# First layer's projection: weight quarters, q stores and modulation pieces issued by items of the tile loop

## The chip, the core and the metric

The kernel runs on one core of one Trainium2 chip. The time is the device time of one execution in microseconds; of several runs the median counts. A core has TensorE (PE in the profile, PEld for its weight loads), VectorE (DVE), ScalarE (ACT), GpSimd (POOL) and SyncE (SP), each with its own queue of instructions; SP issues nearly all loads and stores here.

## The reference, cut to what matters

Two layers of a generator work on 1024 latent and 256 context tokens of width 1024. The first is windowed attention, the second latent attention:

```python
for i in range(DEPTH):                       # DEPTH = 2
    shift_x, scale_x, gate_x = adaln(c, ada_w[i], ada_b[i])
    shift_c, scale_c, gate_c = adaln(c_ctx, ada_w[i], ada_b[i])
    hx = rms_norm(x, norm_g[i]) * (1.0 + scale_x[:, None]) + shift_x[:, None]
    hc = rms_norm(ctx, norm_g[i]) * (1.0 + scale_c) + shift_c
    ...
    x = x + gate_x[:, None] * yx

def window_gqa(hx, hc, w_in, ...):
    q, k, v, g = jnp.split(h @ w_in, ...)    # 1024, 256, 256, 1024 columns
    qx = apply_rope(qx, cos, sin)
    kx = apply_rope(kx, cos, sin)
    ...
    yx = (ox * jax.nn.silu(gx)) @ w_out
```

The change lies in the first layer's product `h @ w_in` and in what runs beside it: `silu(c) @ ada_w` for the first layer's gate and for the whole second layer.

## The kernel before, in words

**Split precision.** Each operand of a product is kept as a high and a low part. `split` (L117 to L121) makes them: ACT casts the value to the high part (L120), and VectorE or GpSimd subtracts it for the low part (L121). A product is three matmuls (L125, L126, L127).

**Items.** `w_in` is cut into ten blocks of 256 columns (`blocks`). Block 0 (v) runs first, token pair by token pair. Then a list `order` of items (block, token group, column half) sets the rest. Blocks 1, 3, 5 and 6 are q, block 7 is k, blocks 2, 4, 8 and 9 are the gate. An item with token group 1 or 2 is 24 matmuls of 512 columns; one with group 0 (the context tokens, both halves) is 48 of 256. So a block is five items, written here as 3,0,0, then 3,1,0, 3,1,1, 3,2,0 and 3,2,1. Blocks 1 to 7 run one after another, 8 and 9 interleaved. `proj_t` (from L428) does an item: the matmuls into one of six PSUM banks, then what empties the bank.

**q tiles.** For a q item DVE multiplies the bank by the cosine (L468) and shuffles it (L469), POOL multiplies by the sine (L470) and adds (L472). The function `rest`, called one item later, splits the sum into a staging tile (ACT L120, DVE L121) and stores it with four DMAs (L487). A gate tile is one ACT instruction (L443) and a store (L446, L448).

**Weights.** `fetch(bi)` brings a block's weights: four quarters of 256 KB, each loaded through a ring of three staging buffers (`stg`), then split by ACT and POOL into one of two weight buffers (`wst`). The call for block b+1 is made at block b's first item, all four quarters at once, so the fourth load must wait until POOL has split the first quarter. From here on "quarter 0 to 3 of block 4" names them.

**Modulation.** `ada_vec` is a generator for eight jobs. A job is 512 columns of `ada_w` in eight pieces of 256 KB (128 rows each), 64 pieces in all, loaded through a ring of four buffers (L341). DVE multiplies a piece by the condition and adds it up (L360, L362), once for the token condition and once for the context's; jobs 6 and 7 have only one. A finished job is summed over partitions by PE (`ada_sum`, L373, one or two matmuls), copied by ACT (L377) or added by DVE (L379); for jobs 2 to 5 four transposes on PE follow (`ada_end`, L392), and small additions (L167, L170). One item lies between the last piece and the sum, and one between the sum and the transposes, counted by `later` and `next_item`. One step of the generator was one DVE instruction; the tile loop took 2, 5 or 6 steps per item, and the next load was called in the same step that used the piece's buffer last.

**What sets the order.** The code above is not yet the order on the engines. A scheduler puts each engine's instructions in a fixed order by the dependences between them, and moves loads and DVE work ahead of where the code calls them. On the chip each engine follows its own order, and waits at an instruction until its inputs and its buffer are there.

Of the kernel before, what the change touches and what calls it, by code (L numbers as in the profile page):

```python
# [59 lines left out]
def kernel(ctx: ExitStack, tc: tile.TileContext, t, out, dbg=None):  # L60
    nc = tc.nc
# [11 lines left out]
    q0_d = dpool.tile([4, 64, 2, NT, 512], F32, name="q0_d")  # L73
# [148 lines left out]
    def load_w(dst, src, stage, nk, n, lo_eng=None, col0=0, k0=0):  # L222

        per = max(1, 512 // n)
        for k in range(k0, nk, per):
            st = shp(stage.next(), per, n)
            load(out=st, in_=src[k * 128 : (k + per) * 128, col0 : col0 + n].rearrange("(k p) n -> p k n", p=128))
            split(dst[:, 0, k : k + per, :], dst[:, 1, k : k + per, :], st, lo_eng or nc.gpsimd)
# [37 lines left out]
    blocks = [1280, 0, 1536, 256, 1792, 512, 768, 1024, 2048, 2304]  # L266
    wt = {}

    def fetch(bi, eng=None):
        wt[bi] = r_at(wst[bi % 2], 2, 8, 256)  # L270
        load_w(wt[bi], w_in, stg, 8, 256, lo_eng=eng, col0=blocks[bi])

    def fetch0(h):
        wt[0] = r_at(wst[0], 2, 8, 256)
# [36 lines left out]
        ada0.set_cols(mt[:, :, 32:34], 0, h)  # L311


    due = []
    item = [0]

    def later(d, fn):
        due.append((item[0] + d, fn))

    def next_item():  # L320
        item[0] += 1
        todo = [x for x in due if x[0] <= item[0]]
        due[:] = [x for x in due if x[0] > item[0]]
        for _, fn in todo:
            fn()

    def ada_vec():
        stage = Ring(F, [14, 16, 18, 20], 512)
        acc = Ring(F, [22, 24, 26, 28], 512)
        tmp = Ring(F, [30, 32], 512)  # L330
        for b in tmp.bufs:
            nc.gpsimd.memset(b[0:33], 0.0)
        jobs = [(ada0, 4), (ada0, 5), (ada1, 2), (ada1, 3), (ada1, 0), (ada1, 1), (ada1, 4), (ada1, 5)]
        pieces = [(a, cb, k) for a, cb in jobs for k in range(8)]
        ws = {}

        def fetch_piece(i):
            if i < len(pieces):
                a, cb, k = pieces[i]
                ws[i] = stage.next()  # L340
                load(out=ws[i], in_=t["ada_w"][a.layer, k * 128 : k * 128 + 128, cb * 512 : cb * 512 + 512])  # L341

        for i in range(4):
            fetch_piece(i)
        i = 0
        for a, cb in jobs:
            nw = 1 if a.layer == 1 and cb >= 4 else 2
            accs = [acc.next() for _ in range(nw)]
            m = tmp.next()
            if cb >= 4:  # L350
                for c in range(nw):
                    load(
                        out=m[32 * c : 32 * c + 1],
                        in_=t["ada_b"][a.layer, cb * 512 : cb * 512 + 512].partition_broadcast(1),
                    )
            for k in range(8):
                w = ws.pop(i)
                for c in range(nw):
                    if k == 0:
                        nc.vector.tensor_scalar_mul(accs[c], w, sc[:, k, c : c + 1])  # L360
                    else:
                        nc.vector.scalar_tensor_tensor(accs[c], w, sc[:, k, c : c + 1], accs[c], ALU.mult, ALU.add)  # L362
                    if c == nw - 1:
                        fetch_piece(i + 4)
                    yield
                i += 1
            later(1, lambda a=a, cb=cb, accs=accs, m=m: ada_sum(a, cb, accs, m))

    def ada_sum(a, cb, accs, m):
        ps = pss()  # L370
        n = len(accs)
        for c in range(n):
            nc.tensor.matmul(ps[32 * c : 32 * c + 1], const[:, 0:1], accs[c], start=True, stop=True)  # L373
        for c in range(n):
            r = slice(32 * c, 32 * c + 1)
            if cb < 4:
                nc.scalar.copy(m[r], ps[r])  # L377
# [44 lines left out]
    def proj_t(bi, gp, c):  # L422
# [51 lines left out]
        def rest():  # L474
            q = shp(qst.next(), 2, 512)
            if c0 == 1024:
                for e in range(2):
                    es = slice(64 * e, 64 * e + 64)
                    nc.vector.tensor_add(q[0:64, e], a[es], r[es])
                    kh = kT[:, 2 * c + e, t0 : t0 + 512]  # L480
                    split(kh[0:64], kh[64:128], q[0:64, e])
                return
            split(q[:, 0].bitcast(F32R), q[:, 1].bitcast(F32R), a)
            for e in range(2):
                for s in range(2):
                    o0 = e * 256 + c * 128
                    load(  # L487
                        out=q0_d[c0 // 256, :, s, t0 // 128 : t0 // 128 + 4, o0 : o0 + 128],
                        in_=shp(q[64 * e : 64 * e + 64, s], 4, 128),
                    )  # L490

        return rest

# [189 lines left out]
    def steps(g, n=200):  # L683
        for _ in range(n):
            next(g, None)
# [61 lines left out]
    for bi, gp, c in order:  # L747
        if bi + 1 < 10 and bi + 1 not in started:
            started.add(bi + 1)
            fetch(bi + 1)  # L750
        next_item()
        steps(ada_steps, 200 if (bi, gp) == (8, 0) else 6 if blocks[bi] >= 1536 else 2 if gp else 5)
        if (bi, gp, c) == (9, 2, 0):
            load2(out=mask, in_=t["mask"])
            load2(out=gx, in_=gate_d[0, 0, :].partition_broadcast(128))
            load2(out=gc, in_=gate_d[0, 1, :].partition_broadcast(128))
        if (bi, gp) == (8, 0):
            units[0].prep_q()
            units[0].prep()
            units[1].prep_q()  # L760
        if (bi, gp) == (9, 0):
            units[1].prep()
            units[2].prep_q()
            for h in range(4):
                units[0].score(h)
        r = proj_t(bi, gp, c)
        if rest:
            rest()
        rest = r
        if bi >= 8 and gp != 1:  # L770
            for _ in range(2):
                next(wo_fill, None)

    units[1].score(0)
    units[1].score(1)
    tq = iter([(u, c) for u in units for c in range(u.m)])
# [755 lines left out]
```

## Time and profile before

| | |
|---|---|
| runs | 1644.03 us median of 3 (1641.09 to 1647.05) |
| profiled execution | 1647.77 us, of it the span 1645.9 us |
| mean granted clock of TensorE | 0.99 |
| busy shares | PE 96%, DVE 59%, ACT 50%, POOL 48% |
| matmuls at L125, L126, L127 | 608.1, 599.2 and 597.0 us busy |
| modulation on DVE (L362) | 98 instructions, 87.7 us |
| read and written in HBM | 129.04 MB and 46.15 MB, 106 GB/s over the span |

Times in rows of the profile are counted from the start of the span. A row of a timeline gives start, length, engine, line and operation, the tile written and the tiles read, and in brackets how long the engine had been idle before and what ended that. `arena_f` and `arena_r` are the two large arrays on chip, in which all buffers lie; `PB` is PSUM.

### The profile page before, as it was taken

The numbers are of one execution on the slowest core, as the hardware profiler recorded it, in microseconds if no ns is written. First come the engines' busy times: TensorE is split into PE (matmuls) and PEld (weight loads), VectorE is DVE, ScalarE is ACT, GpSimd is POOL, SyncE is SP. The second block draws the span as 40 slices with busy tenths as digits, with TensorE's granted clock in tenths as the row PEclk, the third lists the DMA queues.
The fourth block names the chain that finished last, engine by engine and source line by source line (L and its number), as shares of the span: only waits on it lengthen the run. The fifth ranks groups of instructions, "written<-read, shape, count | busy, mean of one in ns | idle before, by whom it ended". The sixth has DMA issues, their size and how long they took to land.

```text
span 1645.9 us, 23722 instructions
## 1 busy us (share of the span) xinstructions
PE 1587.9 (96%) x8156; PEld 1215.5 (74%) x8156; DVE 964.1 (59%) x1972; ACT 825.2 (50%) x1779; POOL 792.5 (48%) x776
## 2 busy tenths in 40 slices
PE   6899999999999999998999999999999999999998
PEld 2687778887878888878887887566756756666687
DVE  1797853539888888869454015655555455455354
ACT  3622112249777777777333334555555555555421
POOL 1444426224453333345254423686676777668510
PEclk9899999999999999999999999999999999999999
DMA  8557665364343333334127713111111111122151
GB/s 280 165 154 204 180 206 141 94 178 124 93 119 94 91 90 90 90 113 160 52 90 251 222 61 103 61 55 33 39 40 34 45 40 35 49 77 69 47 160 65
DMA packets 127202, 176.75 MB, mean 107 GB/s; under 512 B 11100, under 2 KB 69084, under 8 KB 127080
## 3 DMA queue, kind: packets, MB, share of 16 engines
q1 hardware_dynamic: 124920, 171.12, 34.4%
q10 hardware_dynamic: 2160, 4.11, 0.8%
q8 instruction: 64, 1.05, 0.3%
q14 instruction: 58, 0.48, 0.1%
HBM read 129.04 MB, written 46.15 MB: 106 GB/s over the span
## 4 chain that ended last, share of the span: by engine, by line
PE 70%; DVE 11%; ACT 6%; issue 6%; POOL 3%; DMA 3%; SPq 0%; ACTq 0%; DVEq 0%; POOLq 0%
PE PB L125 15%; PE PB L127 15%; PE PB L126 15%; PE PB L1205 9%; PE PB L1171 4%; PE PB L607 3%; PE PB L597 3%; DVE arena_f L362 2%; DVE arena_r L121 2%; PE PB L569 2%; DVE arena_f L576 1%; PE PB L570 1%; ACT arena_f L579 1%; DMA arena_f<-ada_w 1%; ACT arena_r L120 1%
## 5 line engine op out<-in xcount | busy, mean ns | idle before, releaser
L125 PE MATMUL PB<-arena_r 128*128 128x512 f32 (+3 forms) x1632 | 608.1, 373 | 5.7 <-ACT arena_r L204 3.8
L126 PE MATMUL PB<-arena_r 128*128 128x512 f32 (+3 forms) x1632 | 599.2, 368 | 4.0 <-DVE arena_r L206 3.6
L127 PE MATMUL PB<-arena_r 128*128 128x512 f32 (+3 forms) x1632 | 597.0, 368 | 0.2 <-DVE arena_r L121 0.2
L125 PEld LDWEIGHTS PB<-arena_r 128*128 128x128 f32 (+1 forms) x1632 | 311.2, 191 | 95.3 <-issue 30.3
L1197 POOL TENSOR_TENSOR arena_f<-arena_f 128x512 f32<-128x512 f32 x252 | 326.9, 1297 | 76.4 <-ACT arena_f L1190 61.3
L127 PEld LDWEIGHTS PB<-arena_r 128*128 128x128 f32 (+1 forms) x1632 | 310.9, 191 | 50.3 <-issue 0.9
L126 PEld LDWEIGHTS PB<-arena_r 128*128 128x128 f32 (+1 forms) x1632 | 312.2, 191 | 45.9 <-DVE arena_r L206 4.7
L1190 ACT ACTIVATE arena_f<-PB 128x512 f32<-128x512 f32 x320 | 188.9, 597 | 126.6 <-PE PB L127 114.7
L1175 DVE TENSOR_REDUCE arena_f<-PB 128x1 f32<-128x1280 f32 x128 | 190.5, 1488 | 105.4 <-PE PB L1171 102.9
L121 DVE TENSOR_TENSOR arena_r<-PB,arena_r 128x512 fp32r<-128x512 f32 (+4 forms) x255 | 162.3, 644 | 114.8 <-ACT arena_r L120 113.1
L121 POOL TENSOR_TENSOR arena_r<-arena_f,arena_r 128x512 fp32r<-128x512 f32 x84 | 117.6, 1412 | 153.5 <-ACT arena_r L120 106.5
L120 ACT CAST arena_r<-PB 128x512 fp32r<-128x512 f32 (+4 forms) x255 | 137.7, 549 | 66.6 <-PE PB L597 27.8
L576 DVE CUSTOM_DVE_ANT_0 arena_f<-PB,arena_f,small 128x256 f32<-128x256 f32 (+1 forms) x288 | 145.8, 523 | 28.1 <-PE PB L570 21.9
L1205 PE MATMUL PB<-arena_f 128*64 128x512 f32 x640 | 157.1, 600 | 0.0
L579 ACT ACTIVATE arena_f<-arena_f,small 128x640 f32<-128x640 f32 (+2 forms) x160 | 119.3, 747 | 28.8 <-DVE small L578 27.9
L120 ACT CAST arena_r<-arena_f 128x512 fp32r<-128x512 f32 (+2 forms) x132 | 78.3, 609 | 105.5 <-DMA arena_f<-a_w_in 21.3
L607 PE MATMUL PB<-arena_r 128*128 128x512 f32 x336 | 123.3, 441 | 4.3 <-ACT arena_f L618 3.2
L597 PE MATMUL PB<-ident,arena_f 128*128 128x128 f32 x672 | 110.6, 274 | 1.0 <-ACT arena_f L579 0.8
L1205 PEld LDWEIGHTS PB<-arena_f 128*64 128x64 f32 x640 | 43.5, 136 | 80.9 <-issue 79.7
L1171 PE MATMUL PB<-arena_r 96*128 96x512 f32 (+1 forms) x384 | 99.8, 368 | 2.0 <-DVE arena_f L1175 1.9
L362 DVE SCALAR_TENSOR_TENSOR arena_f<-arena_f,small 128x512 f32<-128x512 f32 x98 | 87.7, 942 | 17.7 <-DMA arena_f<-ada_w 17.5
L597 PEld LDWEIGHTS PB<-ident,arena_f 128*128 128x128 f32 x672 | 83.3, 140 | 19.3 <-ACT arena_f L579 4.7
(149 smaller groups left out, 1768.7 us busy)
## 6 DMA issues: line engine op xcount, KB each, us to landing
arena_r<-q_d SPq DMA_DIRECT2D x80, 256.0 KB
arena_f<-ada_w SPq DMA_DIRECT2D x68, 256.0 KB
arena_f<-a_w_in SPq DMA_DIRECT2D x40, 256.0 KB
q_d<-arena_f SPq DMA_DIRECT2D x80, 128.0 KB
arena_f<-x SPq DMA_DIRECT2D x16, 512.0 KB
qn_d<-arena_f SPq DMA_DIRECT2D x16, 512.0 KB
arena_r<-qn_d SPq DMA_DIRECT2D x32, 256.0 KB
arena_f<-ada_w SPq DMA_DIRECT2D x14, 512.0 KB
```

Of the source, the lines that this page charges most:

```text
L120: nc.scalar.copy(hi, src)
L121: (lo_eng or nc.vector).tensor_sub(lo, src, hi.bitcast(F32))
L125: nc.tensor.matmul(o, ah, bh, start=first, stop=False)
L126: nc.tensor.matmul(o, al, bh, start=False, stop=False)
L127: nc.tensor.matmul(o, ah, bl, start=False, stop=last)
L597: nc.tensor.transpose(pt[:, h, :], self.Ps[h][:, ci * 128 : ci * 128 + 128], ident)
L607: nc.tensor.matmul(self.pv, V[:, self.chunks[ci], self.g, :], PT[:, s], start=ci == 0 and s == 0, stop=ci == self.m - 1 and s == 1,)
L1171: nc.tensor.matmul(psm[:, n0 : n0 + n], self.qT[0:96, 0, b * 128 : b * 128 + 128], kt[0:96, 0, n0 : n0 + n], start=True, stop=True,)
L1175: nc.vector.reduce_max(self.mx[:, 96 + b : 97 + b], psm[:, 0:TOK], AX.X, negate=True)
L1190: nc.scalar.activation(E, S, AF.Exp)
L1197: eng.tensor_add(self.acc, self.acc, E)
L1205: nc.tensor.matmul(self.pv[p : p + 64], Vq[:, c, self.h % 4, :], self.E.pop(c), start=c < 2, stop=c >= NT - 2)
```

## The change

Four things are written anew, and no arithmetic changes.

1. `fetch` loads quarters 0 to 2 at its call. One item later it splits quarter 0, loads quarter 3, and splits quarters 1 and 2; two items later it splits quarter 3.
2. A step of `ada_vec` is now a whole piece, both of its DVE instructions. The next load into its buffer is called one item later. The loop takes one step per item in the x items of q and k blocks and two in all others; the step that once drained the generator before blocks 8 and 9 is gone, so jobs 6 and 7 reach into them.
3. The four stores of a q tile are called one item after its split.
4. `next_item` is called first in an item, ahead of the next fetch; it is also called for the token pairs before the loop, and after it until nothing is due.

```diff
-    def fetch(bi, eng=None):
+    def fetch(bi):
+
         wt[bi] = r_at(wst[bi % 2], 2, 8, 256)
-        load_w(wt[bi], w_in, stg, 8, 256, lo_eng=eng, col0=blocks[bi])
+        src = w_in[:, blocks[bi] : blocks[bi] + 256].rearrange("(k p) n -> p k n", p=128)
+        got = []
+
+        def get(i):
+            got.append(shp(stg.next(), 2, 256))
+            load(out=got[i], in_=src[:, 2 * i : 2 * i + 2, :])
+
+        def cut(i):
+            ks = slice(2 * i, 2 * i + 2)
+            split(wt[bi][:, 0, ks, :], wt[bi][:, 1, ks, :], got[i], nc.gpsimd)
+
+        def second():
+            cut(0)
+            get(3)
+            cut(1)
+            cut(2)
+
+        for i in range(3):
+            get(i)
+        later(1, second)
+        later(2, lambda: cut(3))
...
-                    if c == nw - 1:
-                        fetch_piece(i + 4)
-                    yield
+                later(1, lambda i=i: fetch_piece(i + 4))
+                if k == 7:
+                    later(1, lambda a=a, cb=cb, accs=accs, m=m: ada_sum(a, cb, accs, m))
                 i += 1
-            later(1, lambda a=a, cb=cb, accs=accs, m=m: ada_sum(a, cb, accs, m))
+                yield
...
-            for e in range(2):
-                for s in range(2):
...
+            def store():
+                for e in range(2):
+                    for s in range(2):
...
+            later(1, store)
...
     for bi, gp, c in order:
+        next_item()
         if bi + 1 < 10 and bi + 1 not in started:
             started.add(bi + 1)
             fetch(bi + 1)
-        next_item()
-        steps(ada_steps, 200 if (bi, gp) == (8, 0) else 6 if blocks[bi] >= 1536 else 2 if gp else 5)
+        steps(ada_steps, 1 if gp and blocks[bi] < 1536 else 2)
...
+    while due:
+        next_item()
```

What this makes of the engines' orders shows at three places. Up to the sum of job 1 on PE, in block 2, all engines have the old order. The lines of the new kernel are 22 to 26 higher, and its loads of quarters are L291 instead of L227.

**SP at the end of block 2.** Rows: `a_w_in` is a quarter of weights, `ada_w` a piece of modulation, `g_d` a store of a gate tile, `gate_d` the store of a finished gate job, `q_d` a store of q. Before:

```order
L446 DMA g_d<-arena_f 128x512 x2
L385 DMA gate_d<-arena_f 1x512 x2
L227 DMA arena_f<-a_w_in 128x2x256
L341 DMA arena_f<-ada_w 128x512 x3
L227 DMA arena_f<-a_w_in 128x2x256
L446 DMA g_d<-arena_f 128x512
L341 DMA arena_f<-ada_w 128x512
L227 DMA arena_f<-a_w_in 128x2x256 x2
```

Now:

```order
L468 DMA g_d<-arena_f 128x512 x2
L291 DMA arena_f<-a_w_in 128x2x256 x3
L468 DMA g_d<-arena_f 128x512
L291 DMA arena_f<-a_w_in 128x2x256
L407 DMA gate_d<-arena_f 1x512 x2
L363 DMA arena_f<-ada_w 128x512 x4
```

In both the quarters are quarter 3 of block 4 and quarters 0 to 2 of block 5, and the four pieces are 28 to 31 of the 64 (the second half of job 3). Before, three of the pieces stood ahead of block 5's quarters; now all four stand behind its quarter 2, and the gate stores too.

**DVE at the head of block 3.** `TENSOR_SCALAR` and `SCALAR_TENSOR_TENSOR` are modulation, L121 from `PB` is the split of item 3,0,0, L468 and L469 (now L490 and L491) take a q tile off PSUM. Before:

```order
L362 SCALAR_TENSOR_TENSOR arena_f<-arena_f,small 128x512 x14
L121 TENSOR_TENSOR arena_f<-PB,arena_f 128x512
L468 TENSOR_TENSOR arena_f<-PB,arena_f 128x512
L469 STREAM_SHUFFLE arena_f<-PB 128x512
L360 TENSOR_SCALAR arena_f<-arena_f,small 128x512 x2
L362 SCALAR_TENSOR_TENSOR arena_f<-arena_f,small 128x512 x2
L121 TENSOR_TENSOR arena_f<-arena_f 128x512
L362 SCALAR_TENSOR_TENSOR arena_f<-arena_f,small 128x512 x4
```

Now:

```order
L384 SCALAR_TENSOR_TENSOR arena_f<-arena_f,small 128x512 x7
L121 TENSOR_TENSOR arena_f<-PB,arena_f 128x512
L384 SCALAR_TENSOR_TENSOR arena_f<-arena_f,small 128x512 x6
L490 TENSOR_TENSOR arena_f<-PB,arena_f 128x512
L491 STREAM_SHUFFLE arena_f<-PB 128x512
L384 SCALAR_TENSOR_TENSOR arena_f<-arena_f,small 128x512
L121 TENSOR_TENSOR arena_f<-arena_f 128x512
```

The first rows are job 3 in both (its pieces 25 to 31). Before, job 4 followed among the q tiles of block 3; now no modulation stands among the rest of them, and job 4 comes behind the block, with job 5 behind it, ahead of the first q tile of block 5.

**ACT at the end of block 3.** L120 to `arena_f` is the cast of a q tile, to `arena_r` that of a quarter of weights; L443 (now L465) is a gate tile of block 4, L377 (now L399) the copies of a job's sum. Before:

```order
L120 CAST arena_f<-arena_f 128x512
L120 CAST arena_r<-arena_f 128x512 x2
L120 CAST arena_f<-arena_f 128x512
L443 ACTIVATE arena_f<-PB 128x512 x2
L377 COPY arena_f<-PB 1x512 x2
```

Now:

```order
L120 CAST arena_f<-arena_f 128x512
L120 CAST arena_r<-arena_f 128x512 x3
L120 CAST arena_f<-arena_f 128x512
L465 ACTIVATE arena_f<-PB 128x512
L399 COPY arena_f<-PB 1x512 x2
```

The two casts to `arena_f` are items 3,2,0 and 3,2,1. The copies were those of job 3, with two gate tiles ahead of them; now they are those of job 2, with one. On PE the sum and the transposes of job 2 stand before items 4,1,0 and 4,1,1 (those of job 3 stood before 4,1,1 and 4,2,0). POOL's order between the same two q tiles has changed likewise: its splits of block 5's four quarters now all stand between the sums of 3,2,0 and the multiply of 3,2,1, where quarter 0 stood ahead of the sum of 3,2,0 before.

More of the change, by code (lines that the diff above doesn't have):

```diff
@@ L267, with later, next_item @@
     wt = {}
[L269 to L271 removed]
+    due = []
+    item = [0]
+    def later(d, fn):
+        due.append((item[0] + d, fn))
+    def next_item():
+        item[0] += 1
+        todo = [x for x in due if x[0] <= item[0]]
+        due[:] = [x for x in due if x[0] > item[0]]
+        for _, fn in todo:
+            fn()
+    def fetch(bi):
+        wt[bi] = r_at(wst[bi % 2], 2, 8, 256)
+        src = w_in[:, blocks[bi] : blocks[bi] + 256].rearrange("(k p) n -> p k n", p=128)
[15 more added lines that the diff above has]
+        later(2, lambda: cut(3))
     def fetch0(h):
@@ L772 @@
                 next(wo_fill, None)
+    while due:
+        next_item()
     units[1].score(0)
```

20 lines of the change are left out of this document (5 added, 15 removed).

## The prediction

> **What bounds the kernel now.** I read the page's first part, then the waits of PE over the whole span, then windows of 10 us over the first layer's projection, then the timeline of each engine around the two windows that fall out.
>
> ```profile
> PE 1587.9 (96%) x8156; PEld 1215.5 (74%) x8156; DVE 964.1 (59%) x1972; ACT 825.2 (50%) x1779; POOL 792.5 (48%) x776
> ...
> PE PB L187 <- DVE arena_f L180: 8.6, 8, 2.7
> PE PB L301 <- DMA arena_f<-ada_w: 7.8, 5, 4.6
> PE PB L392 <- ACT arena_f L377: 7.6, 2, 4.1
> ```
>
> The first line is the share of busy time, the others are PE's longest waits (total us, times, longest). PE is busy for 96% of the span, so nothing but a wait of PE can be won. The changed code touches only the stage that runs from about 88 to 358 us. Of the three waits, L187 and L301 belong to work that the change leaves alone. Only the last, 7.6 us in two pieces at L392 (the four transposes of a finished modulation job), lies in that stage.
>
> ```profile
> 190.00:200.00 10.00, 6.57 (x28) 4.43 (x24) 3.91 (x8) 3.81 (x7) 7.71 (x6) 0.98 0.52 137
> 200.00:210.00 10.00, 9.36 (x32) 7.53 (x33) 5.39 (x10) 1.73 (x3) 0.00 (x0) 0.67 0.95 276
> 220.00:230.00 10.00, 6.45 (x32) 5.32 (x31) 3.81 (x7) 2.26 (x4) 1.26 (x1) 0.85 0.86 276
> 300.00:310.00 10.00, 10.00 (x46) 8.29 (x45) 7.63 (x11) 4.00 (x7) 3.95 (x4) 1.00 0.13 39
> ```
>
> Columns: stretch, its length, busy us of PE, PEld, DVE, ACT, POOL with counts, granted clock, DMA share, GB/s. The last row is an undisturbed stretch: 46 matmuls, clock 1.00. The other three lose matmuls to idle time and, from 200 us, to a lower granted clock.
>
> ```profile
> 200.64 0.63 PE L392 MATMUL PB<-ident,arena_f 33*128 33x33 f32 x4 [4.07 <-ACT arena_f L377]
> 201.20 0.79 PE L125 MATMUL PB<-arena_r 128*128 128x512 f32 x1
> ...
> 203.50 0.63 PE L127 MATMUL PB<-arena_r 128*128 128x512 f32 x1
> ...
> 206.06 0.61 PE L127 MATMUL PB<-arena_r 128*128 128x512 f32 x1
> ...
> 206.97 0.40 PE L127 MATMUL PB<-arena_r 128*128 128x512 f32 x1
> ...
> 209.02 0.39 PE L127 MATMUL PB<-arena_r 128*128 128x512 f32 x1
> ...
> 225.30 0.43 PE L392 MATMUL PB<-ident,arena_f 33*128 33x33 f32 x4 [3.55 <-ACT arena_f L377]
> 225.67 0.50 PE L125 MATMUL PB<-arena_r 128*128 128x512 f32 x1
> ...
> 227.27 0.63 PE L125 MATMUL PB<-arena_r 128*128 128x512 f32 x1
> ...
> 230.26 0.48 PE L126 MATMUL PB<-arena_r 128*128 128x512 f32 x1
> ```
>
> PE's timeline: start, length, line, operation, and in brackets the idle time before it. From 203.50 to 206.06 six matmuls start 0.427 us apart; from 206.97 to 209.02 nine start 0.228 us apart. So after the 4.07 us wait some twelve matmuls (201.20 to 206.06) ran at half pace, which costs 12 x 0.20 = 2.4 us. After the 3.55 us wait seven (227.27 to 230.26) did so: 1.4 us. The two waits and what follows them cost 4.07 + 2.4 + 3.55 + 1.4 = 11.4 us. That is all that this stage can give back, 0.7% of the time.
>
> ```profile
> 168.18 0.68 DVE L468 TENSOR_TENSOR arena_f<-PB,arena_f 128x512 f32<-128x512 f32 x1
> 192.73 0.68 DVE L468 TENSOR_TENSOR arena_f<-PB,arena_f 128x512 f32<-128x512 f32 x1
> 197.82 0.62 ACT L120 CAST arena_f<-arena_f 128x512 fp32r<-128x512 f32 x1 [5.12 <-POOL arena_f L472]
> 198.47 1.08 ACT L443 ACTIVATE arena_f<-PB 128x512 f32<-128x512 f32 x2
> 199.44 1.15 ACT L377 COPY arena_f<-PB 1x512 f32<-1x512 f32 x2
> ...
> 223.55 0.62 ACT L120 CAST arena_r<-arena_f 128x512 fp32r<-128x512 f32 x1 [8.07 <-DMA arena_f<-a_w_in]
> 224.08 1.17 ACT L377 COPY arena_f<-PB 1x512 f32<-1x512 f32 x2
> ...
> 218.08 1.61 SPq L227 DMA_DIRECT2D arena_f<-a_w_in  x3
> ```
>
> Why PE waited: the transposes need the copies L377 on ACT, and ACT takes its work in order. Ahead of the first pair of copies stands the cast of the last q tile of block 3 (item 3,2,1). It waited for POOL, and POOL for DVE, which took the first q tile of block 3 off PSUM at 168.18 and the fourth at 192.73: 24.6 us for three rounds, 8.2 us each, while PE makes a tile in 24 x 0.227 = 5.4 us. Ahead of the second pair stands a weight cast whose load, issued at 218.08, took 5.5 us to be cast.
>
> **The change part by part.** Every instruction stays; the same work is issued in another order. The static orders of all engines agree up to about 142.7 us (the sum of job 1 is the first matmul to move), so up to there the time is the old one: 0. The weight quarters of blocks 1 to 3 and the extra calls at the start and at the end are in this part or move nothing: 0, with neither gain nor loss left to bound. The q stores of the later blocks stand one tile further back on SP; only SP's own loads queue behind them, which are counted below, and their staging buffer is wanted two tiles later: 0, and at most one tile (5.4) if they hold back a quarter.
>
> What goes: both L392 waits at their old places, -11.4 us. The second one's cause is gone in the order: no modulation loads stand between SP's gate stores and the last quarter for block 6 any more. The 14 multiply-adds of job 4, which stood among block 3's q tiles on DVE, are gone from there as well, so its rounds shrink. A round without them is shown by block 6 of before:
>
> ```profile
> 268.96 0.69 DVE L468 TENSOR_TENSOR arena_f<-PB,arena_f 128x512 f32<-128x512 f32 x1 [0.63 <-PE PB L127]
> 274.40 0.69 DVE L468 TENSOR_TENSOR arena_f<-PB,arena_f 128x512 f32<-128x512 f32 x1
> ...
> 271.76 1.29 POOL L472 TENSOR_TENSOR arena_f<-arena_f 128x512 f32<-128x512 f32 x1
> ...
> 279.77 0.37 SPq L227 DMA_DIRECT2D arena_f<-a_w_in  x1
> 283.30 1.29 POOL L121 TENSOR_TENSOR arena_r<-arena_f,arena_r 128x512 fp32r<-128x512 f32 x1 [0.59 <-ACT arena_r L120]
> ```
>
> From the multiply that takes a tile off PSUM (268.96) to the next one 5.44 us pass, the same as PE's pace, and the rope sum on POOL ends 4.09 us after it (271.76 + 1.29). So lag that exists at the head of a q block is neither gained nor lost in it. The last two rows are the round trip of a fourth weight quarter: issued when POOL has freed its buffer, 4.82 us until POOL has split it (283.30 + 1.29 - 279.77).
>
> What comes: a wait of SP. It now issues quarter 2 of block 5 ahead of pieces 28 to 31 of the modulation, and this quarter's buffer is freed by POOL's split of quarter 3 of block 4.
>
> ```profile
> 155.51 0.57 SPq L385 DMA_DIRECT2D gate_d<-arena_f  x2
> 156.19 0.40 SPq L227 DMA_DIRECT2D arena_f<-a_w_in  x1
> 156.68 2.66 SPq L341 DMA_DIRECT2D arena_f<-ada_w  x3
> ...
> 160.38 0.62 ACT L120 CAST arena_r<-arena_f 128x512 fp32r<-128x512 f32 x1 [10.36 <-DMA arena_f<-a_w_in]
> ...
> 161.07 1.28 POOL L121 TENSOR_TENSOR arena_r<-arena_f,arena_r 128x512 fp32r<-128x512 f32 x1 [10.28 <-ACT arena_r L120]
> ...
> 156.25 4.06 DVE L362 SCALAR_TENSOR_TENSOR arena_f<-arena_f,small 128x512 f32<-128x512 f32 x6
> 161.08 6.46 DVE L362 SCALAR_TENSOR_TENSOR arena_f<-arena_f,small 128x512 f32<-128x512 f32 x8 [0.77 <-DMA arena_f<-ada_w]
> ```
>
> Before, SP issued the quarter at 156.19 and pieces 28 to 30 right behind it, at 156.68; the quarter was cast at 160.38 and split by 162.35, and DVE went on with piece 28 at 161.08, 4.4 us after its issue. In the changed order the gate store (L385) stands behind, so the quarter goes out at 155.5 and is split by 155.5 + (162.35 - 156.19) = 161.7. Only then SP issues quarter 2 (0.4), the gate stores (0.6) and piece 28, at 162.7. It lands at 162.7 + 4.4 = 167.1, 6 us later than before. Queued behind it on DVE: one multiply-add (0.7), the subtraction of item 3,0,0 (0.6), six multiply-adds (4.06, the row at 156.25), then the first q tile of block 3, at 172.5 instead of 168.18. With rounds of 5.44 the sum of the third tile ends on POOL at 172.5 + 10.9 + 4.1 = 187.5. Behind it POOL now has all four splits of block 5 before the fourth tile: first split 1.3, then the round trip 4.8, 193.6; multiply and add of the tile 2.7, 196.3. ACT: from the cast to the end of the copies took 197.82 to 200.59 with two gate tiles between, now there is one (0.5 less): the copies of job 2 end at 198.6.
>
> ```profile
> 189.87 1.03 PE L373 MATMUL PB<-arena_f,small 128*1 128x512 f32 x4
> 190.83 0.50 PE L125 MATMUL PB<-arena_r 128*128 128x512 f32 x1
> ```
>
> When does PE want them? It began item 4,1,1 at 190.83, with three sums (0.96 each, 189.87 to 190.83) and one set of transposes (0.37, 225.30 to 225.67) behind it since 142.7. In the changed order the transposes of job 2 stand right before this item with two sums and no transposes behind: 190.83 - 0.96 - 0.37 = 189.5. **PE waits 198.6 - 189.5 = 9.1 us.** Bounds: a load as quick as in the round trip above (4.82 less the cast's 0.62 and the split's 1.29, so 2.9 us) takes 1.3 off the quarter and 1.5 off the piece; one as slow as the 5.5 us at 218.08 adds 1.3 to the first quarter and 2.6 to the one in POOL's queue: 6 to 13. I stay at 9.1, where each load has its own row. The pace after the wait costs 2.4 us by the first old wait and 1.4 by the second; I take the longer wait's, and as upper end 1.0 more, 3.4.
>
> The Trainium skill (TensorE: Matmul & The Clock Gate, Part 1) says that PE falls to half clock after an idle window of some 3.4 us and comes back after about 3.4 us of work. That would make the restart 1.7 us instead of 2.4 and the whole sum 0.7 us smaller; half pace agrees with 0.427 against 0.228, but the stretch from 201.20 to 206.06 is 4.9 us long, so the row decides.
>
> Later places. The transposes of job 3 stand before item 5,1,0; block 4 has no rope chain, and the copies stand behind one weight cast whose load is free of the pieces: 0, and 1 at most. Those of job 4 (before 6,1,1) and job 5 (before 7,2,1) stand behind q tiles again, of blocks 5 and 6, with POOL's four splits ahead of the fourth tile. There the head of the block is late by 1 to 4 us instead of 12, since the job's pieces are spread better. I take 0.7 us each; ends 0 and 3.55, the nearest wait that the trace has. They would be too short to add a slow stretch.
>
> Sum: -11.4 + 9.1 + 2.4 + 0.7 + 0.7 = **+1.5 us**. On the profiled execution, 1647.77 (1645.9 of it the span), that is 1649.3. This execution lies 3.7 us above the median of the runs, 1644.03, so I forecast 1645.5: a wait moved, not removed. The terms' ends give -11.4 + 6 + 1.4 = -4 and -11.4 + 13 + 3.4 + 1 + 7.1 = +13.
>
> **The rivals.** *The waits go* (chance 0.22). If piece 28 came as early as before and the quarter's round trip in POOL's queue were short, the fourth tile would be cast 6 to 9 us earlier and PE would find its copies ready: -11.4, 1632.6; with half of the wait left, 1638. For it: rounds without multiply-adds keep PE's pace. Against: no row above has a load back in under 2.9 us, and two of them stand one behind the other.
>
> *The later transposes stall in earnest* (0.20), the slower side. Place: before 6,1,1 and 7,2,1. From a lag of some 4 us at the head of block 5 on, each wait passes 3.5 us and brings its slow stretch, 3.55 + 1.4 each, in place of my 0.7: +1.5 + 8.5 = 10, 1654. For it: job 5's sixteen operations now stand in front of block 5's first q tile, and SP's pieces 44 to 47 behind two waits for POOL. Against: those pieces have the whole of block 4 to catch up.
>
> *The order hardly matters* (0.08): the loads are hoisted by the scheduler before and after, as the common first 142 us show, and the lag comes from DVE and POOL alone; then one wait replaces two at about equal cost, 1644.
>
> **How the numbers follow.** My forecast has 0.50, the rivals 0.22, 0.20 and 0.08. What a measurement of this kernel can tell from no change is about 0.3%, 4.9 us. Of the forecast 0.02 lies faster than that and 0.04 slower (its ends), of the first rival 0.19 faster, of the second 0.17 slower; the third lies within. Faster 0.21, slower 0.21, same 0.58. The range takes in the half-kept wait (1638) and most of the way to the forecast's upper end, and leaves out the full gain (1632.6) and the full loss (1654), about 0.1 each: 1635 to 1652.
>
> **What would show it.** In the changed profile: piece 28's multiply-add on DVE waits for ada_w until about 167; the first q tile of block 3 leaves PSUM near 172; rounds of 5.4 us; one wait of PE at the transposes (now L414) of 6 to 10 us near 190, followed by a granted clock near 0.7 in that window, and none at 200 to 230. Wrong if PE waits nowhere between 180 and 300 us, or if two or more waits over 3 us stand there.

## The result, and the profile after

The changed kernel takes 1656.41 us (median of 4 runs, 1654.87 to 1659.26), the kernel before 1644.4 (4 runs). The ratio is 1.0076, 95% interval 1.0053 to 1.0099: 9 to 16 us slower, where 1645.5 and no change were forecast. The profiled execution has a span of 1653.9 us, 8.0 more than the one before.

The loss stands in the stage that was changed. From the first matmul of item 1,1,0 to the first matmul of the scores, PE's timeline gives 260.1 us before (97.53 to 357.62) and 269.8 after (96.52 to 366.34), 9.7 more. Ahead of the stage the profiled execution after is 1.0 us shorter, and behind it 0.7, which leaves the 8.0 of the spans. PE's busy time in the page and its waits over the span:

```profile
PE 1586.5 (96%) x8156; PEld 1214.7 (73%) x8156; DVE 953.9 (58%) x1972; ACT 826.2 (50%) x1779; POOL 790.5 (48%) x776
...
PE PB L414 <- ACT arena_f L399: 17.1, 2, 10.2
```

L414 is the old L392, the transposes. Their waits were 7.6 us, the longest 4.1; they are 17.1 now, still two. The busy time hides this, since it moved by 1.4 us. Windows of the stage (columns as in the prediction):

```profile
190.00:200.00 10.00, 1.54 (x6) 1.33 (x7) 3.65 (x7) 3.36 (x6) 5.39 (x5) 0.62 0.69 190
220.00:230.00 10.00, 10.00 (x64) 8.90 (x63) 9.71 (x17) 0.59 (x1) 0.35 (x1) 1.00 0.77 247
300.00:310.00 10.00, 3.84 (x12) 3.10 (x13) 7.43 (x14) 3.94 (x7) 2.25 (x2) 0.58 0.08 20
310.00:320.00 10.00, 10.00 (x42) 8.17 (x41) 6.61 (x10) 3.11 (x6) 7.45 (x6) 0.91 0.23 73
```

From 190 to 200 us PE does 6 matmuls, four of them the small transposes, where it did 28. The stretch from 220 to 230, with its 3.55 us wait before, now runs without a wait and at clock 1.00. And from 300 to 310, undisturbed before with 46 matmuls, PE now does 12. PE's timeline at both places:

```profile
198.46 0.63 PE L414 MATMUL PB<-ident,arena_f 33*128 33x33 f32 x4 [10.19 <-ACT arena_f L399]
199.02 0.79 PE L125 MATMUL PB<-arena_r 128*128 128x512 f32 x1
...
202.60 0.41 PE L127 MATMUL PB<-arena_r 128*128 128x512 f32 x1
...
306.16 0.63 PE L414 MATMUL PB<-ident,arena_f 33*128 33x33 f32 x4 [6.96 <-ACT arena_f L399]
306.72 0.79 PE L125 MATMUL PB<-arena_r 128*128 128x512 f32 x1
...
311.58 0.53 PE L127 MATMUL PB<-arena_r 128*128 128x512 f32 x1
...
314.71 0.39 PE L125 MATMUL PB<-arena_r 128*128 128x512 f32 x1
```

A wait of 10.19 us before the transposes of job 2, in front of item 4,1,1, and one of 6.96 before those of job 5, in front of item 7,2,1. Item 4,1,1 then took 199.02 to 206.29, 7.27 us in place of 5.44, and item 7,2,1 took 306.72 to 314.71, 7.99 us. With these slow stretches the two places cost 10.19 + 1.83 + 6.96 + 2.55 = 21.5 us. The same sum before is 4.07 + 2.61 + 3.55 + 1.74 = 12.0 us (items 201.20 to 209.25 and 225.67 to 232.85). So 9.5 of the 9.7 us are told by these waits.

**The first wait** came as the prediction worked it out. Rows of SP, DVE, POOL and ACT, in order of time:

```profile
161.27 0.37 SPq L291 DMA_DIRECT2D arena_f<-a_w_in  x1
162.44 1.78 SPq L363 DMA_DIRECT2D arena_f<-ada_w  x4
166.91 0.75 DVE L384 SCALAR_TENSOR_TENSOR arena_f<-arena_f,small 128x512 f32<-128x512 f32 x1 [8.22 <-DMA arena_f<-ada_w]
172.27 0.68 DVE L490 TENSOR_TENSOR arena_f<-PB,arena_f 128x512 f32<-128x512 f32 x1
186.22 1.29 POOL L494 TENSOR_TENSOR arena_f<-arena_f 128x512 f32<-128x512 f32 x1
192.39 1.26 POOL L121 TENSOR_TENSOR arena_r<-arena_f,arena_r 128x512 fp32r<-128x512 f32 x1 [0.75 <-ACT arena_r L120]
196.25 0.62 ACT L120 CAST arena_f<-arena_f 128x512 fp32r<-128x512 f32 x1 [3.93 <-POOL arena_f L494]
197.26 1.15 ACT L399 COPY arena_f<-PB 1x512 f32<-1x512 f32 x2
```

SP got rid of block 5's quarter 2 at 161.27 and issued the next pieces from 162.44. DVE, 8.22 us idle, used the first at 166.91 and took the first q tile of block 3 off PSUM at 172.27. The third tile's sum ended on POOL at 187.51 (186.22 + 1.29), the four splits at 193.65, the fourth tile was cast at 196.25, and the copies of job 2 ended at 198.41.

**The second wait** has another story. Rows of block 6 and the head of block 7:

```profile
254.74 2.64 SPq L511 DMA_DIRECT2D q_d<-arena_f  x4
257.48 2.56 SPq L483 DMA_DIRECT2D q_d<-arena_f  x4
260.14 3.05 SPq L363 DMA_DIRECT2D arena_f<-ada_w  x3
...
259.02 0.69 DVE L490 TENSOR_TENSOR arena_f<-PB,arena_f 128x512 f32<-128x512 f32 x1 [0.22 <-PE PB L127]
...
264.46 2.33 DVE L384 SCALAR_TENSOR_TENSOR arena_f<-arena_f,small 128x512 f32<-128x512 f32 x3 [4.05 <-DMA arena_f<-ada_w]
...
269.49 0.68 DVE L490 TENSOR_TENSOR arena_f<-PB,arena_f 128x512 f32<-128x512 f32 x1
...
274.87 1.53 DVE L384 SCALAR_TENSOR_TENSOR arena_f<-arena_f,small 128x512 f32<-128x512 f32 x2
276.31 0.68 DVE L490 TENSOR_TENSOR arena_f<-PB,arena_f 128x512 f32<-128x512 f32 x1
...
279.40 1.30 POOL L121 TENSOR_TENSOR arena_r<-arena_f,arena_r 128x512 fp32r<-128x512 f32 x1
...
282.64 1.11 DVE L121 TENSOR_TENSOR arena_f<-arena_f 128x512 fp32r<-128x512 f32 x1 [4.34 <-ACT arena_f L120]
...
287.07 0.68 DVE L490 TENSOR_TENSOR arena_f<-PB,arena_f 128x512 f32<-128x512 f32 x1
...
291.82 2.65 SPq L511 DMA_DIRECT2D q_d<-arena_f  x4
294.52 0.61 SPq L363 DMA_DIRECT2D arena_f<-ada_w  x1
...
297.55 0.75 DVE L384 SCALAR_TENSOR_TENSOR arena_f<-arena_f,small 128x512 f32<-128x512 f32 x1 [2.97 <-DMA arena_f<-ada_w]
298.31 0.69 DVE L490 TENSOR_TENSOR arena_f<-PB,arena_f 128x512 f32<-128x512 f32 x1
...
301.80 1.28 ACT L120 CAST arena_r<-arena_f 64x512 fp32r<-64x512 f32 x2 [7.94 <-DVE arena_f L501]
304.55 0.33 ACTq L781 DMA_DIRECT2D arena_f<-mask  x1
304.93 1.18 ACT L399 COPY arena_f<-PB 1x512 f32<-1x512 f32 x2 [1.85 <-DVE arena_f L490]
```

At 259.02 DVE was on time: it waited 0.22 us for PE before it took the first q tile of block 6. Behind the tile's shuffle and one small addition stood a multiply-add of the modulation, and that waited 4.05 us for a piece. SP had issued the piece only at 260.14, behind the eight stores of items 5,2,1 and 6,0,0 (L511, L483). The first of these could go when ACT had cast item 5,2,1, at 254.72, and the eight took 5.2 us to issue.

The next tiles left PSUM 10.5, 6.8 and 10.8 us apart, where the kernel before had 5.44 (268.96 to 274.40). Only the first of these three rounds holds a long wait for a piece. The second is longer by its two multiply-adds, which stand between the split of one tile and the multiply of the next (274.87). In the third, POOL has one split of a weight quarter (279.40) between the tile's multiply and its sum, and two multiply-adds behind DVE's split of 282.64 took 3.48 us beside POOL's other splits (283.68, shown in the last section). Added up, the tiles are 11.7 us behind PE's pace of 5.44 by then, and 5.0, 1.4 and 5.3 of it are from the three rounds.

At the head of block 7 a piece behind the store of item 6,2,1 (291.82) is issued at 294.52 and used at 297.55, and only then the first k tile leaves PSUM. This adds no lag: from the fourth q tile to the first k tile it is 11.2 us, and it was 12.0 in the kernel before (280.21 to 292.23, 1.5 of it a wait for PE). ACT casts that tile at 301.80, waits with the load of the attention's mask until 304.55, and copies job 5's sum at 304.93, though PE had made it by 293.5. DVE had finished job 5 by 230.6; the pieces in between belong to jobs 6 and 7, whose sums PE wants only in block 9.

### The profile page after: what moved, and what is told of

Same layout as the page of the kernel before. It is cut to its first block, busy times and chain, and to the rows that moved or that the text cites. A ratio compares the mean times of both kernels' runs of the same rounds, so it can differ in the third digit from the quotient of the medians.

```text
span 1653.9 us, 23717 instructions
## 1 busy us (share of the span) xinstructions
PE 1586.5 (96%) x8156; PEld 1214.7 (73%) x8156; DVE 953.9 (58%) x1972; ACT 826.2 (50%) x1779; POOL 790.5 (48%) x776
## 3 DMA queue, kind: packets, MB, share of 16 engines
q8 instruction: 64, 1.05, 0.3%
## 4 chain that ended last, share of the span: by engine, by line
PE 68%; DVE 10%; issue 7%; ACT 6%; POOL 5%; DMA 3%; SPq 0%; ACTq 0%; DVEq 0%; POOLq 0%
PE PB L125 14%; PE PB L127 14%; PE PB L126 14%; PE PB L1234 9%; PE PB L1200 4%; PE PB L633 3%; PE PB L623 3%; DVE arena_r L121 2%; PE PB L595 2%; PE PB L596 2%; DVE arena_f L384 1%; DVE arena_f L602 1%; ACT arena_f L605 1%; DVE arena_f L201 1%; DMA arena_f<-ada_w 1%
## 5 line engine op out<-in xcount | busy, mean ns | idle before, releaser
L121 DVE TENSOR_TENSOR arena_r<-PB,arena_r 128x512 fp32r<-128x512 f32 (+4 forms) x255 | 162.1, 644 | 115.5 <-ACT arena_r L120 113.8
L121 POOL TENSOR_TENSOR arena_r<-arena_f,arena_r 128x512 fp32r<-128x512 f32 x84 | 116.2, 1395 | 153.5 <-ACT arena_r L120 98.7
L120 ACT CAST arena_r<-PB 128x512 fp32r<-128x512 f32 (+4 forms) x255 | 137.8, 549 | 65.2 <-PE PB L623 30.1
L120 ACT CAST arena_r<-arena_f 128x512 fp32r<-128x512 f32 (+2 forms) x132 | 78.5, 609 | 101.9 <-DMA arena_f<-b_w_in 20.4
L656 POOL TENSOR_TENSOR arena_f<-arena_f 128x256 f32<-128x256 f32 x39 | 28.7, 736 | 135.8 <-ACT arena_f L644 132.3
```

Of the source, the lines that this page charges most:

```text
L120: nc.scalar.copy(hi, src)
L121: (lo_eng or nc.vector).tensor_sub(lo, src, hi.bitcast(F32))
```

## The experiments

All waits are those of PE at the transposes, in the profiled execution; "stage" runs from item 1,1,0 to the first scores as above. The kernel before was run beside each.

| kernel | waits, us | stage, us | median, us | ratio to before, 95% interval |
|---|---|---|---|---|
| before | 4.07, 3.55 | 260.1 | 1644.4 | |
| after | 10.19, 6.96 | 269.8 | 1656.4 | 1.0076 (1.0053 to 1.0099) |
| e1 pacing undone | 3.61, 3.34 | 259.2 | 1644.1 | 0.9991 (0.9981 to 1.0001) |
| e2 after, transposes two later | 6.73 | 259.4 | 1642.7 | 0.9981 (0.9969 to 0.9994) |
| e3 before, one later | 1.44 | 249.6 | 1637.7 | 0.9947 (0.9932 to 0.9962) |
| e4 fourth staging buffer | 6.55, 6.91 | 266.0 | 1650.3 | 1.0021 (1.0008 to 1.0033) |
| e5 q stores on ACT | 7.59, 1.40 | 259.8 | 1647.7 | 1.0005 (0.9989 to 1.0021) |
| e6 mask later | 9.14, 5.62 | 268.2 | 1653.3 | 1.0041 (1.0025 to 1.0057) |
| e7 gate blocks three | 5.02, 3.92, 3.27 | 265.6 | 1650.7 | 1.0032 (1.0021 to 1.0043) |
| e8 stores on ACT, two later | none | 249.1 | 1636.8 | 0.9938 (0.9915 to 0.9960) |
| e9 before, two later | none | 247.7 | 1633.7 | 0.9930 (0.9910 to 0.9950) |
| e10 e9 with a third row buffer | none | 247.6 | 1630.9 | 0.9911 (0.9897 to 0.9924) |

Without a wait the stage takes 247.6 to 249.1 us. The kernel before stands 12 above that and the changed one 22, which is again what their waits and slow stretches add up to.

**e1: the pacing undone, fetch and stores kept.**

```diff
-                later(1, lambda i=i: fetch_piece(i + 4))
-                if k == 7:
-                    later(1, lambda a=a, cb=cb, accs=accs, m=m: ada_sum(a, cb, accs, m))
-                i += 1
-                yield
+                    if c == nw - 1:
+                        fetch_piece(i + 4)
+                    yield
+                i += 1
+            later(1, lambda a=a, cb=cb, accs=accs, m=m: ada_sum(a, cb, accs, m))
...
-        steps(ada_steps, 1 if gp and blocks[bi] < 1536 else 2)
+        steps(ada_steps, 200 if (bi, gp) == (8, 0) else 6 if blocks[bi] >= 1536 else 2 if gp else 5)
```

> The new weight fetch and the later q stores are kept, the old pacing of the modulation (steps in multiply-adds, sum called behind the job) is put back. Theory 1, the pacing alone moves instructions: the time of the kernel before, 1644 (1641 to 1648), PE waits at the transposes of 4.1 and 3.6 us. Rival, the fetch or the stores cost something of their own: between 1648 and 1657.

Measured 0.9991 of the kernel before, waits 3.61 and 3.34. The rows of all five engines, with buffers and semaphores, are those of the kernel before: the scheduler makes nothing of the new fetch and the later stores. The other way round, the changed kernel with the old fetch and the old place of the stores has the changed kernel's rows on every engine (it was not timed). So three of the four points of the change move nothing; the pacing does all. This pair is also one program measured twice: 1644.1 (11 runs) and 1646.4 (19 runs), which is how far two medians lie apart with no change at all.

**e2 and e3: the transposes later.** In the changed kernel by two items (e2, shown), in the kernel before by one (e3, with 2 in place of 3):

```diff
-        later(1, lambda: ada_end(a, cb, m, n))
+        later(1 if cb >= 4 else 3, lambda: ada_end(a, cb, m, n))
```

> The changed kernel with each job's transposes two items later. Their inputs are ready at 198.5 us (job 2) and 306.2 us (job 5); PE gets there at 188.3 + 2 x 5.44 = 199.2 and 299.2 + 10.9 = 310.1. Theory 1, all of the loss is these waits with their slow stretches (10.2 + 1.8 + 7.0 + 2.6 = 21.5 us): no wait at the transposes, 1656.4 - 21.5 = 1635. Rival, the lag of the q tiles is a lag of its own and turns up at the next thing that PE needs (the weights of block 9, split by POOL behind those tiles at 319 us, PE there at about 304 to 312, or a PSUM bank): a wait of 4 us or more at L125, 1640 to 1645.

> The kernel before with each job's transposes one item later (5.4 us, against waits of 4.1 and 3.6). Theory 1: both waits and their slow stretches go (4.1 + 2.6 + 3.6 + 1.7 = 12.0 us), 1644.4 - 12.0 = 1632.4. Rival, the wait moves on to another matmul: 1638 to 1645.

e2, the wait that is left:

```profile
304.34 0.64 PE L414 MATMUL PB<-ident,arena_f 33*128 33x33 f32 x4 [6.73 <-ACT arena_f L399]
```

The first wait went, the second stayed, so the rival held in its main point, though not in its place: the wait is not at weights or a bank but at the same transposes. The arithmetic of the expectation was wrong: without the first wait PE is 12 us earlier everywhere and comes to job 5's transposes at 297.6, not at 310.1. The copies end at 304.29, nearly where they ended before (306.1). The chain behind them has its own pace and does not hurry when PE does.

e3 is 8.7 us faster than the kernel before run beside it (1646.4 - 1637.7), where 12.0 was expected; its stage is 10.5 us shorter. A part of the wait of job 4, in front of item 5,1,1, is left:

```profile
220.11 0.43 PE L392 MATMUL PB<-ident,arena_f 33*128 33x33 f32 x4 [1.44 <-ACT arena_f L377]
```

**e4: a fourth staging buffer for the weights.**

```diff
-    stg = Ring(F, [4, 6, 8], 512)
+    stg = Ring(F, [4, 6, 8, 46], 512)
-    ev = Ring(F, [38, 40, 42, 44, 46], 512)
+    ev = Ring(F, [38, 40, 42, 44], 512)
```

> The changed kernel with a fourth staging buffer for the weight quarters (taken from the ring of five that the q and gate tiles use). The rows of PE, DVE, ACT and POOL stay as they are up to block 9; what goes is SP's wait for POOL ahead of piece 28 and the round trip of the fourth quarter within POOL's row. Theory 1, these two make the first wait: piece 28 is used on DVE near 161 instead of 166.9, the first q tile of block 3 leaves PSUM near 166 instead of 172.3, the wait at the transposes of job 2 falls from 10.2 to some 3.6 us. For the second wait, theory 2a (POOL's splits with their round trip pass the lag from block to block): 7.0 falls below 2, in all -14, 1642. Theory 2b (SP's pieces behind the q stores, no matter what POOL does): it stays near 7, in all -8, 1648. Rival to theory 1: first wait 8 or more.

DVE, POOL and PE:

```profile
163.96 0.75 DVE L384 SCALAR_TENSOR_TENSOR arena_f<-arena_f,small 128x512 f32<-128x512 f32 x1 [4.28 <-DMA arena_f<-ada_w]
184.51 5.45 POOL L121 TENSOR_TENSOR arena_r<-arena_f,arena_r 128x512 fp32r<-128x512 f32 x4
...
194.77 0.63 PE L414 MATMUL PB<-ident,arena_f 33*128 33x33 f32 x4 [6.55 <-ACT arena_f L399]
302.35 0.63 PE L414 MATMUL PB<-ident,arena_f 33*128 33x33 f32 x4 [6.91 <-ACT arena_f L399]
```

The piece came 2.95 us earlier (163.96 against 166.91), and the four splits took 5.45 us in one row instead of 6.19 (187.46 to 193.65): together 3.7, and the first wait is 3.6 shorter. So both causes are real, but they carry a third of the wait, not the two thirds that were expected. SP's four piece loads went out at 158.57, not at 156: they still stand behind the quarters and the gate stores. What remains of the wait is the distance from DVE's late first tile over the four splits to the copies, which no extra buffer shortens. The second wait did not move (6.91): theory 2a is out. The stage is 3.8 us shorter; the ratios, 1.0021 against 1.0076, say 9 us, with 3.3 as the least that the two intervals allow.

**e5: the q stores on ACT's queue.**

```diff
-                        load(
+                        load2(
                             out=q0_d[c0 // 256, :, s, t0 // 128 : t0 // 128 + 4, o0 : o0 + 128],
```

> The changed kernel with the q stores of the later token groups issued by ACT's queue in place of SP's, so that SP's piece loads stand behind no store that waits for DVE. Theory 2b (the lag of block 6 is made by pieces of the modulation that SP may issue only behind the stores of the tile before, 3 to 4 us of waiting on DVE in each round): the rounds of block 6 fall from 10.5, 6.8 and 10.8 us towards 5.5, and the second wait (7.0 us, before item 7,2,1) falls below 2. The stores' issue, 4 x 0.65 us, now stands on ACT ahead of the copies of job 2, so the first wait grows from 10.2 to about 13. In all about 1650. Rival (POOL's splits or the k tiles make the lag): the rounds stay, the second wait stays at 7 or grows by 2.6, 1657 to 1662.

PE and DVE:

```profile
196.28 0.64 PE L414 MATMUL PB<-ident,arena_f 33*128 33x33 f32 x4 [7.59 <-ACT arena_f L399]
299.18 0.43 PE L414 MATMUL PB<-ident,arena_f 33*128 33x33 f32 x4 [1.40 <-ACT arena_f L399]
...
260.54 3.31 DVE L384 SCALAR_TENSOR_TENSOR arena_f<-arena_f,small 128x512 f32<-128x512 f32 x3 [1.05 <-DMA arena_f<-ada_w]
...
266.82 0.68 DVE L490 TENSOR_TENSOR arena_f<-PB,arena_f 128x512 f32<-128x512 f32 x1
...
273.61 0.68 DVE L490 TENSOR_TENSOR arena_f<-PB,arena_f 128x512 f32<-128x512 f32 x1
...
280.17 0.68 DVE L490 TENSOR_TENSOR arena_f<-PB,arena_f 128x512 f32<-128x512 f32 x1
```

The second wait falls from 6.96 to 1.40 and DVE's wait for the piece from 4.05 to 1.05 us. Theory 2b holds for the first round, 8.7 us in place of 10.5: SP had issued a piece that DVE needed behind stores. The third round gained more, 6.6 in place of 10.8, and it had no wait for a piece. There the edit did something that the expectation did not name: it also changed the orders of DVE and POOL in block 6. The split that stood between the third tile's multiply and sum now stands in the fourth tile, and no multiply-add follows DVE's split in the third round. How much of the second wait is SP's queue and how much these orders, e5 does not separate. The first wait shrank, where it was to grow: POOL's splits now stand around the fourth tile's multiply and sum, not all ahead of them.

**e6: the mask's load behind the copies of job 5.**

```diff
-    mask = f_at(0, 384)
+    mask = f_at(2, 384)
-    gr = Ring(F, [1.5, 2.5, 46], 256)
+    gr = Ring(F, [0, 1, 46], 256)
```

> The changed kernel with the attention's mask placed 2 KB further on, over a part of the cosine table that is read last; its load then stands on ACT's queue behind the copies of job 5, not ahead of them. Nothing else moves. Theory: the load held ACT for 1.85 us (it waits for the multiply of item 7,1,1), so the second wait falls from 7.0 to 5.1, 1654. Rival: no change, 1656, if something else holds the copies as long.

ACT and PE:

```profile
300.58 1.28 ACT L120 CAST arena_r<-arena_f 64x512 fp32r<-64x512 f32 x2 [7.99 <-DVE arena_f L501]
301.89 1.18 ACT L399 COPY arena_f<-PB 1x512 f32<-1x512 f32 x2
...
303.12 0.64 PE L414 MATMUL PB<-ident,arena_f 33*128 33x33 f32 x4 [5.62 <-ACT arena_f L399]
```

The copies now follow the k tile's cast at once (300.58 + 1.28 = 301.86); the 1.85 us of holding are gone. The second wait is 5.62, 1.3 shorter, and the time 1653.3. So the mask's load is a part of that wait, and the smaller one. The first wait, 9.14, was not to move. Its slow stretch is longer in turn (2.98 in place of 1.83), so the first place costs what it did, 12.1 us. Two loads of gate tiles on SP moved ahead too (to 303.3 us), so the mask's load is not all that the edit moved.

**e7: three pieces per item in the gate blocks.**

```diff
-        steps(ada_steps, 1 if gp and blocks[bi] < 1536 else 2)
+        steps(ada_steps, 3 if blocks[bi] >= 1536 else 1 if gp else 2)
```

> The changed kernel with 3 pieces instead of 2 in each item of a gate block (15 per gate block, as the kernel before did; the q blocks stay at 6). Theory 2c (the loss comes from the pieces that the gate blocks no longer take, which then fall into blocks 5 and 6, two q blocks in a row): no wait at the transposes of job 5, waits of about 4 at those of job 2 and job 3 as in the kernel before, about 1645. Rival (whole pieces instead of single multiply-adds, or the sums one item earlier, make the loss): 1650 or more.

PE's three waits:

```profile
199.17 0.63 PE L414 MATMUL PB<-ident,arena_f 33*128 33x33 f32 x4 [5.02 <-ACT arena_f L399]
223.45 0.44 PE L414 MATMUL PB<-ident,arena_f 33*128 33x33 f32 x4 [3.92 <-ACT arena_f L399]
257.66 0.43 PE L414 MATMUL PB<-ident,arena_f 33*128 33x33 f32 x4 [3.27 <-ACT arena_f L399]
```

The rival. The two waits of the kernel before are back (jobs 3 and 4), and job 5 keeps one of 3.27. How many pieces a gate item takes decides before which item the transposes meet late copies; it does not make the copies early. Here block 5 has multiply-adds among its q tiles (rounds of 9.5, 5.8 and 5.8 us) and gets the lag, and block 6 has none and keeps 5.4 to 5.8. Why this cadence is worse than the old one, with as many pieces per gate block, was not taken further.

**e8: both cures.** The edits of e5 and e2 together.

> The changed kernel with the q stores on ACT's queue and the transposes two items later. Theory 2b: the second wait, which stayed at 6.7 us with the transposes two later alone since the chain behind it is slower than PE, goes as well; the first has 2 us left at most. About 1656.4 - 20 = 1636. Rival: a wait of 6 to 7 us stays before item 8,1,1, 1643.

No wait is left, 0.9938. The second wait, which neither PE's delay nor a fourth buffer touched, is gone with both edits together: e5's new orders, and PE asking two items later.

**e9 and e10: the kernel before, transposes two later.**

> The kernel before with each job's transposes two items later. With one item later 1.4 us of waiting were left (before item 5,1,1) and 1637.7; one more item is 5.4 us. Theory 1: no wait of PE at the transposes, as with e8, and about 1636. Rival: the wait turns up at another matmul, 1638 or more.

> As e9, with a third buffer for a job's summed rows (from the ring of five of the q and gate tiles, which is left with four), so that no bias row of job 7 is loaded into the rows that the transposes of job 5 still have to read. PE's order is that of e9. Theory 1: no wait at the transposes, 1634 to 1637. Rival: the smaller ring holds up a q or gate tile, 1638 or more.

e9 changes a part of the computation: the bias row of job 7 is loaded at 247.3 us into the rows that the transposes of job 5 read at 249.1, so job 5's columns are not the reference's. e10 gives the rows a third buffer:

```diff
-    ev = Ring(F, [38, 40, 42, 44, 46], 512)
+    ev = Ring(F, [38, 40, 42, 44], 512)
...
-        tmp = Ring(F, [30, 32], 512)
+        tmp = Ring(F, [30, 32, 46], 512)
...
-        later(1, lambda: ada_end(a, cb, m, n))
+        later(1 if cb >= 4 else 3, lambda: ada_end(a, cb, m, n))
```

It takes 1630.9 us, 0.9911 of the kernel before, with no wait at the transposes: three lines on the old pacing beat both kernels.

## Why the prediction was wrong

- **What bounds the kernel: right.** PE's waits at the transposes are all that the stage has to give or lose. Every experiment's stage follows them, down to 247.6 us where there are none.
- **What goes: right.** Nothing of PE waits between 200 and 299 us. The forecast took off 11.4, the items say 12.0.
- **The first wait: right, step by step.** Forecast and measured: piece on DVE 167.1 and 166.91; first q tile 172.5 and 172.27; third sum 187.5 and 187.51; splits done 193.6 and 193.65; copies done 198.6 and 198.41. PE came a little earlier than thought (188.27 for 189.5; 1.0 us of it stood already at item 1,1,0), so 10.19 in place of 9.1. The slow stretch cost 1.83, not 2.4. Old waits against this one give +0.0 where +0.1 was forecast: here a wait was moved, not removed.
- **The later transposes: the step that failed.** "I take 0.7 us each" for jobs 4 and 5; measured 0 for job 4 and 6.96 + 2.55 = 9.5 for job 5. This term is the whole loss. Behind it stands the sentence "So lag that exists at the head of a q block is neither gained nor lost in it". It was read from block 6 of the kernel before, with no multiply-add among its tiles, and carried over to a block 6 that has some: jobs 6 and 7, spread by the new pacing, stand between the q tiles. The block began with no lag (259.02) and ended with 11.7 us: from one wait of 4.05 us for a piece behind stores, from the multiply-adds' own time, and from a split of POOL's within the third round. That lag comes with multiply-adds among the tiles is shown by the q blocks that have none: rounds of 5.4 to 5.8 us in block 5 here and in block 6 of e7. e4 excludes the round trip of POOL's fourth quarter; the share of SP's queue stays open (e5).
- **What was left out of the sum.** ACT's order at 7,2,1 has a k tile's casts and the mask's load ahead of the copies. The k tile was counted as a q tile, and the load not at all; it held ACT for 1.85 us (e6).
- **The rivals.** *The waits go* is out with the first wait of 10.19 us. "The later transposes stall in earnest" named two places, of which 7,2,1 had its wait, and a time of 1654, with a chance of 0.20. Its mechanism, lag from the head of block 5, was not the one: block 5's four tiles left PSUM 5.4 to 5.8 us apart (230.55 to 247.09) and 6,1,1 had no wait. So its time came near for another reason than the one it gave. The counter-argument written beside it, that the pieces have the whole of block 4 to catch up, is true of job 5 and misses jobs 6 and 7. "The order hardly matters" was wrong of the pacing and right of the fetch and the stores (e1).
- **The signs.** The piece at 167, the tile at 172, and no wait from 200 to 230 came as said; the clock from 190 to 200 is 0.62 for "near 0.7". Of "two or more waits over 3 us" between 180 and 300, the second began at 299.20, on the edge of the stretch that was named.
- **The sum.** With 9.5 us at job 5 and 0 at job 4 in place of 0.7 + 0.7, the forecast's +1.5 becomes +9.6; the stage says +9.7. The upper end of the terms, +13, had 3.55 for each later place and so held this in all, but the range was cut at 1652 on the chances.

The Trainium skill (TensorE: Matmul & The Clock Gate, Part 1) has PE back at full clock after about 3.4 us of work, 1.7 us lost, an estimate from the page's figure. The shortest slow stretches agree: 199.02 to 202.60 here, 3.6 us, at a cost of 1.83. The row at 306.72 is longer than that one figure: half pace to 311.58, 4.9 us. The Trainium skill says in the same section that the window in which the activity is counted is free-running, and that the same kernel showed 6, 11 or 14 slow matmuls at its start. The 7 to 14 slow ones behind the waits of the runs here fit that.

## What to carry to other kernels

Look at the built order of every engine before pricing an edit: three of four edits here moved no instruction, and all that moved was moved by the fourth, the pacing. When PE waits at a small step with a long chain behind it and nothing urgent ahead of it, put the step later: one number, `later(3)`, was worth more than any attempt to make the chain faster, provided that its buffers live as long. Work of low urgency, as jobs 6 and 7 here, does harm when it is spread among urgent work that an engine takes in order: block 6 fell 11.7 us behind with it. And look at what stands ahead of a load that an engine needs: here eight stores on the same queue, 5.2 us of issue, and 4.05 us of waiting on DVE.

## What was not expected of the hardware

The slow stretch of PE does not follow the length of the wait. Counting 128x512 matmuls that start 0.4 to 0.6 us apart, where 0.23 is the usual: 8 after the wait of 10.19 us, 11 after 6.96, 12 after 4.07 (before), 7 after 3.55 (before, and these began only 1.6 us behind the wait), 8 after 3.27 (e7), 14 after 9.14 (e6), none after 1.44 (e3) and 1.40 (e5). A wait of 4 us can cost more behind it than one of 10.

DVE's multiply-adds slow down beside POOL's work. DVE and POOL after:

```profile
283.68 3.48 DVE L384 SCALAR_TENSOR_TENSOR arena_f<-arena_f,small 128x512 f32<-128x512 f32 x2
...
281.91 4.70 POOL L121 TENSOR_TENSOR arena_r<-arena_f,arena_r 128x512 fp32r<-128x512 f32 x3
```

1.74 us each, against 0.74 for the one at 267.31 us with POOL idle. Of the 98 multiply-adds of the changed kernel, the 78 with POOL idle took 0.73 to 0.75 us, and the 20 beside an instruction of POOL 1.39 on average and 1.78 at most. It was seen in the trace, not tested apart. The Trainium skill (GPSIMD Engine Reference, Specifications) says that the two engines share their SBUF interfaces and contend when a DVE instruction has two SBUF inputs, as these have; the two rows agree with it.
